# Second to sixth modulation: weighted sums over the row tiles moved from the matmul engine to GpSimd

## The chip, the cores and the metric

The kernel runs on one core of one Trainium2 chip, as one program with one launch. The metric is the device time of that core in microseconds (us). A run's time is a little more than the span of its trace, which goes from the first instruction to the last. The engines are called as the profile calls them: PE is the matmul engine (PEld its weight loads), DVE the vector engine, ACT the scalar engine, POOL is GpSimd, and SP is the engine whose queue issues nearly all transfers.

## The reference

One layer of a diffusion backbone over 512 tokens of width 1024, with a context of 256 tokens. What the change touches is the modulation vector: the conditioning vector `c` goes through silu, is multiplied with a weight matrix of 1024 rows and 6 x 1024 columns, a bias is added, and the 6144 numbers are cut into six vectors of 1024.

```python
def adaln(cond, w_mod, b_mod):
    return jnp.split(jax.nn.silu(cond) @ w_mod + b_mod, 6, axis=-1)
...
sh1, sc1, g1, sh2, sc2, g2 = [m[:, None, :] for m in adaln(c, w_mod[l], b_mod[l])]
csh1, csc1, cg1, csh2, csc2, cg2 = adaln(c_ctx, w_mod[l], b_mod[l])
hx = modulate(rmsnorm(x, norm_attn_g[l]), sh1, sc1)
...                       # latent attention and neighbourhood attention, concatenated, projected: mixed
x = x + g1 * mixed
hx2 = modulate(rmsnorm(x, norm_ffn_g[l]), sh2, sc2)
x = x + g2 * hierarchical_moe(hx2, ...)
```

The first two vectors (shift and scale of the first norm) are needed at once, for the tokens and for the context; the kernel computes them at its start. The other four (g1, sh2, sc2, g2, columns 2048 to 6143) are needed for the tokens alone, and late: g1 when the attention output is projected, sh2 and sc2 before the experts, g2 in the experts. The matrix part for these four is 1024 x 4096 numbers, 16 MB in fp32.

## The kernel before, in words

The stages follow one another: the first modulation, the norms and the input projections (to about 110 us of the trace); neighbourhood attention, with the projections of the next heads mixed in (about 110 to 245 us); latent attention with the output projection (to about 370 us); routing (to about 434 us); sixteen experts; the last sums and the last norm.

The change is in the neighbourhood stage. It is a loop over 32 blocks `b`: four pairs of heads `p`, two heads `u`, four tiles of 128 queries `i`. Each block computes scores (L603, L604, on PE), adds the bias to them and takes the row maximum (L609, L469, on DVE), takes the exponential (L616, on ACT), and one block later turns the probabilities (L625, on PE) and copies them out of PSUM. Between these it pulls pieces of the projections of the next pair (L56 to L58, on PE). In the last eight blocks, and in the turns after them, the pieces are those of the latent attention's values, whose weights `w_ukv`, `w_uq` are loaded there.

In every second block, `mod_rest(n)` does one sixteenth of the rest of the modulation: `n` runs over two halves `r` of 2048 columns and eight tiles `k` of 128 rows. It loads 128 x 2048 weights in two pieces of 512 KB into the `raw` buffers, of which there are three and which all weight loads of this stage share (L179), and issues four matmuls of 512 columns. Their stationary side is `sstat[:, k, :]`, 128 rows by 32 columns with the silu of `c` in column 0 and that of `c_ctx` in column 1; each of the four lands on its own 32 columns of PE's array and its own 32 rows of one PSUM bank. After the eighth tile DVE adds the bias row (L524), and the result goes to `mod_d` in DRAM (L525), from which the later stages read it.

The order of the instructions on each engine is not written out by hand in this stage. A planner takes each engine's instructions in about the order of the code, but lets one go ahead whose inputs it expects to be there earlier; so an engine's queue can differ from the code (SP's does, by far). At run time each queue is in order: an instruction that waits holds everything behind it on its engine.

The buffers of the pool `omp` (two of 128 x 2048 fp32, tags `0` and `1`) hold `qst` and `krs` before this stage. Both are stored to DRAM (L422 `qn_dram`, L410 `kr_dram`), and the buffers are idle then until the latent stage puts `omh` and `oml` in them. `zero` is a tile of zeros that is stored ten times to clear `ya_d` (L774).

Of the kernel before, what the change touches and what calls it, by code (L numbers as in the profile page):

```python
# [37 lines left out]
def hybrid_kernel(tc, nc, x_k, x_q, ctx, cvec, w_mod_a, w_mod_b, b_mod_c, b_mod_r, g_ffn_row,  # L38
# [90 lines left out]
    sm = cst.tile([P, 24], F32, name="sm")  # L129
    eps = cst.tile([P, 1], F32, name="eps")  # L130
    ve.memset(eps, EPS)
    lg = cst.tile([P, 4, 20], F32, name="lg")
    lsh = cst.tile([P, 20], F32, name="lsh")
    idx = cst.tile([P, 2, NE], I32, name="idx")
    wsl = cst.tile([P, NE], F32, name="wsl")
# [41 lines left out]
    def load(src, n=1024):  # L177
        r = raw_tile()
        sy.dma_start(r[:, :n], src)  # L179
        return r  # L180
# [317 lines left out]


    ya_d = tc.dram_tile([T + P, D], F32, name="ya_d")  # L500
    zero = nw.tile([P, 512], F32, name="zero")
    ve.memset(zero, 0.0)


    mod_d = tc.dram_tile([2, 4, 512], F32, name="mod_d")
    modf = mod_d.rearrange("r a b -> r (a b)")
    mod_ps = []

    def mod_rest(n):
        r, k = divmod(n, KT)  # L510
        if k == 0:
            br = nw.tile([P, 512], F32, name="br", tag="br", bufs=1)
            ve.memset(br, 0.0)
            rows = br.rearrange("(a b) n -> a b n", b=32)[:, 0, :]
            sy.dma_start(rows, b_mod_r[r])
            mod_ps[:] = bank(7), br, rows
        ps, br, rows = mod_ps
        ws = [load(w_mod_b[r, k, :, q * 1024:(q + 1) * 1024]) for q in range(2)]
        for g in range(4):
            pe.matmul(ps[g * 32:(g + 1) * 32, :], sstat[:, k, :],  # L520
                      ws[g // 2][:, g % 2 * 512:g % 2 * 512 + 512], start=(k == 0), stop=(k == KT - 1),
                      tile_position=(0, g * 32))
        if k == KT - 1:
            ve.tensor_tensor(br, br, ps, op=OP.add)  # L524
            sy.dma_start(mod_d[r], rows)  # L525

    na_heads, na_w, na_ps = {}, {}, {}

# [149 lines left out]

    blocks = [(p, u, i) for p in range(4) for u in range(2) for i in range(4)]
    na_open(0)  # L680
    for j in range(2):
        for i in range(2):
            na_weights(0, j, i)
# [27 lines left out]
    for b, (p, u, i) in enumerate(blocks):  # L711
        w = b % 8
        if w == 0 and p < 3:
            na_open(p + 1)
        s = na_scores(p, u, i)
        nm = na_max(p, u, i, s)
        if p < 3:
            if w in (3, 5, 7):
                for u_ in range(2):
                    na_part(p + 1, w // 2 - 1, u_, 1)  # L720
            if w == 2:
                na_weights(p + 1, 1, 1)
            if w == 4 and p < 2:
                na_weights(p + 2, 0, 1)
            if w == 6:
                for u_ in range(2):
                    na_bias(p + 1, u_)
        if NS[p][w] > 1:
            pull(1)
        if len(turns) >= (2 if b > 24 else 1):  # L730
            na_turn(*turns.pop(0))
        turns.append((p, u, i))
        na_exp(p, u, i, s, nm)
        if w == 0 and p:
            norm_ = normalise_steps(na_ssum[p - 1], nw, onh[:, p - 1, :], onl[:, p - 1, :])
            next(norm_)
        if i % 2:
            mod_rest(p * 4 + u * 2 + i // 2)
        pull(NS[p][w] - (NS[p][w] > 1))
        if w == 0 and p:  # L740
            norm_.send((na_values(p - 1), bank4(4, 5)))
        if w == 1 and p:
            for _ in norm_:
                pass
        if p < 3:
            if w in (2, 4, 6):
                for u_ in range(2):
                    na_part(p + 1, w // 2 - 1, u_, 0)
            if w == 1:
                na_weights(p + 1, 1, 0)  # L750
            if w == 3 and p < 2:
                na_weights(p + 2, 0, 0)
        if b == 23:
            htp.release()
            ml = pool("ml")
            vv = ml.tile([P, 6, 512], F32, name="vv")
            wkh = ml.tile([P, 2, 512], F32R, name="wkh")
            wkl = ml.tile([P, 2, 512], F32R, name="wkl")
            mp = pool("mp")
            ckq = mp.tile([P, 256], F32, name="ckq")  # L760
            qnl = mp.tile([P, 3, T], F32R, name="qnl")
            qnh = mp.tile([P, 3, T], F32R, name="qnh")
            sy.dma_start(ckq, cpk[:, K_QC:K_R])
            krt = mp.tile([P, T + TC], F32, name="krt")
            sy.dma_start(krt[64:96, :], kr_dram)
            uq = [[mp.tile([P, 768], F32R, name=f"uq{c}{i_}") for i_ in range(2)] for c in range(3)]
            mla_weights(0)
            works = works2
        if b == 24:
            mla_weights(1)  # L770
        if w == 7:
            for n in range(2 * p, min(2 * p + 2, 5)):
                for hf in range(2):
                    sy.dma_start(ya_d[n * P:(n + 1) * P, hf * 512:hf * 512 + 512], zero)  # L774
    for tn in turns:
        pull(1)
        na_turn(*tn)
# [290 lines left out]
    rng3 = pool("rng3", side="right")  # L1068
    add_slots(rng3, M1 - R1 - LD)
    wp = pool("wp", side="right")  # L1070
    gs = wp.tile([P, D], F32, name="gs")
    sh = wp.tile([P, D], F32, name="sh")
    sy.dma_start(gs, modf[1:2, 0:1024].to_broadcast([P, D]))
# [754 lines left out]
def _layout(**n):  # L1828
    n = {k: np.asarray(v) for k, v in n.items()}
    c = np.ascontiguousarray  # L1830
    ck_, qr_ = _tokens()
    x = n["x"][0]
    wm, wi = n["w_mod"][0], n["w_in"][0]
    bm = n["b_mod"][0]
    a = {}
    a["x_k"] = c(x[ck_].reshape(4, P, D))
    a["x_q"] = c(x[qr_].reshape(4, P, D))
    a["ctx"] = c(n["ctx"][0].reshape(2, P, D))
    a["cvec"] = c(np.stack([n["c"][0], n["c_ctx"]], -1).reshape(KT, P, 2).transpose(1, 0, 2))

    wa = wm[:, :2048].reshape(4, 2, P, 2, 4, 256).transpose(4, 0, 2, 1, 3, 5)

    w0 = wm[:, :2048].reshape(2, 4, P, 2, KT, P)[:, :, :, :, 0:2].transpose(4, 0, 2, 1, 3, 5)
    a["w_mod_a"] = np.concatenate([w0.reshape(1, 4, P, 1024), wa.reshape(4, 4, P, 1024)[1:]])
    a["w_mod_b"] = c(wm[:, 2048:].reshape(KT, P, 2, 2048).transpose(2, 0, 1, 3))

    bt = np.repeat(bm[:2048].reshape(2, 4, 2, P).transpose(3, 1, 0, 2).reshape(P, 4, 4), 2, axis=2)
    gt = np.repeat(n["norm_attn_g"][0].reshape(4, 2, P).transpose(2, 0, 1), 2, axis=2)
    a["b_mod_c"] = c(np.concatenate([bt, gt], 2))
    a["b_mod_r"] = c(bm[2048:].reshape(2, 4, 512))  # L1850
    a["g_ffn_row"] = c(n["norm_ffn_g"])
    a["g_fin_row"] = c(n["final_norm_g"][None])
    nk0 = 384 + 512 + 256 + 32
    a["w_v"] = c(wi[:, nk0 + 512:].reshape(4, 2, P, 512).transpose(0, 2, 1, 3).reshape(4, P, 1024))
    a["w_kv"] = c(wi[:, 896:1184].reshape(KT, P, 288).transpose(1, 0, 2).reshape(P, KT * 288))
    a["w_ql"] = c(wi[:, :384].reshape(4, 2, P, 384).transpose(0, 2, 1, 3).reshape(4, P, 768))
    qk = np.stack([wi[:, 384:896].reshape(KT, P, 4, P), wi[:, nk0:nk0 + 512].reshape(KT, P, 4, P)])
    a["w_qk"] = c(qk.transpose(3, 0, 2, 1, 4).reshape(4, 2, P, 1024))
    a["g_q"] = c(n["q_a_norm_g"][0].reshape(3, P).T)
    a["g_kv"] = c(n["kv_a_norm_g"][0].reshape(2, P).T)  # L1860
    a["w_uq"] = c(n["w_uq"][0].reshape(3, P, 768))
    a["w_ukv"] = c(n["w_ukv"][0].reshape(2, P, NH, 2, 64).transpose(0, 1, 3, 2, 4).reshape(2, P, 1024))
    i, qr = np.arange(P)[:, None] // 8, np.arange(P)[:, None] % 8
    j, kr = np.arange(256)[None, :] // 8, np.arange(256)[None, :] % 8
    dc, dr = j - i + 7, kr - qr + 7
    ok = (dc >= 0) & (dc < 31)
    a["rel"] = c(np.where(ok, n["na_rel_bias"][0][:, dr, np.clip(dc, 0, 30)], np.float32(0)))
    wo = n["w_out"][0]
    a["w_out_a"] = c(wo[512:].reshape(2, 2, P, 2, 512).transpose(3, 0, 2, 1, 4).reshape(2, 2, P, 1024))
    a["w_out_b"] = c(wo[:512].reshape(4, P, D))  # L1870
    wr = np.concatenate([n["w_router_group"][0], n["w_router_expert"][0]], 1)
    a["w_r"] = c(wr.reshape(KT, P, 20).transpose(1, 0, 2))
    a["b_r"] = c(np.concatenate([n["b_router_group"], n["b_router_expert"]], 1))
    a["w_gate"] = c(n["w_gate"][0].reshape(NE, 2, 4, P, 512).transpose(0, 1, 3, 2, 4).reshape(NE, 2, P, 2048))
    a["w_up"] = c(n["w_up"][0].reshape(NE, 2, 4, P, 512).transpose(0, 1, 3, 2, 4).reshape(NE, 2, P, 2048))
    a["w_down"] = c(n["w_down"][0].reshape(NE, 2, 2, P, D).transpose(0, 1, 3, 2, 4).reshape(NE, 2, P, 2048))
    a["cpk0"], a["cpk"] = _constants()
    return a
# [23 lines left out]
```

## Time and profile before

| | us |
|---|---|
| median of 3 runs | 741.38 |
| lowest, highest | 739.67, 742.3 |
| the profiled execution | 742.79 |
| its span | 740.6 |
| PE busy | 699.0 (94% of the span) |
| DVE busy | 545.6 (74%) |
| ACT busy | 445.9 (60%) |
| POOL busy | 79.6 (11%) |

A PE that is busy is not a PE at its peak: the ends of matmuls are modelled and overlap. What counts on it is the distance from the start of a group of matmuls to the start of the next. An instruction's idle time is put down to what ended it.

### The profile page before, as it was taken

The page shows a single profiled execution, that of the slowest core. Times are in us where ns is not written, and L with a number is a line of the kernel's source. Part 1 is how long each engine was busy: PE and PEld are TensorE (multiplying, and loading weights), DVE is VectorE, ACT ScalarE, POOL GpSimd, SP SyncE. Part 2 cuts the span into 40 slices and gives each one's busy share as a digit, 9 for nine tenths or more (in the row PEclk, how much of TensorE's full clock was granted, in tenths as well). Part 3 has the DMA queues.
Part 4 walks back from the last instruction along what each step waited for, and adds up shares of the span by engine and source line. Part 5 has one row for each costly group of instructions (what it writes and reads, how often), then busy time and mean ns, then how long its engine had stood idle before and what let it go on. Part 6 is the DMA issues. An engine that isn't in the chain of part 4 may idle for free. (4 is left out here: it accounts for less than half of the span.)

```text
span 740.6 us, 10570 instructions
## 1 busy us (share of the span) xinstructions
PE 699.0 (94%) x3982; PEld 521.0 (70%) x3983; DVE 545.6 (74%) x744; ACT 445.9 (60%) x697; POOL 79.6 (11%) x50
## 2 busy tenths in 40 slices
PE   4999999999989999999999559999999999999995
PEld 3679988777755887867668537777777777777773
DVE  5572466756666695656627758999999999999996
ACT  6452365554545565646644437777777777777773
POOL 1010000000000000000010011222222222221320
PEclk9999999999999999999999759999999999999998
DMA  9931238654556821121179859999999999999672
GB/s 322 408 127 43 86 131 263 220 184 142 169 194 205 284 87 43 63 76 48 58 269 344 325 178 355 387 369 373 360 361 356 379 363 364 364 369 380 261 135 113
DMA packets 39622, 176.95 MB, mean 239 GB/s; under 512 B 5288, under 2 KB 6768, under 8 KB 27280
## 3 DMA queue, kind: packets, MB, share of 16 engines
q1 hardware_dynamic: 35168, 164.24, 60.3%
q0 software_dynamic: 4112, 11.92, 7.5%
q8 instruction: 32, 0.52, 0.3%
q14 instruction: 22, 0.18, 0.1%
q10 hardware_dynamic: 288, 0.08, 0.0%
HBM read 163.00 MB, written 15.32 MB: 241 GB/s over the span
## 5 line engine op out<-in xcount | busy, mean ns | idle before, releaser
L1360 DVE TENSOR_TENSOR el<-ew,eh 128x2048 fp32r<-128x2048 f32 (+1 forms) x106 | 220.5, 2086 | 22.0 <-ACT eh L1357 13.2
L1357 ACT CAST eh<-ew 128x1024 fp32r<-128x1024 f32 x190 | 189.7, 1048 | 43.7 <-PE s L58 29.1
L56 PE MATMUL s<-eh,xh 128*96 128x512 f32 x260 | 104.6, 402 | 0.9 <-ACT xh L61 0.9
L58 PE MATMUL s<-eh,xl 128*96 128x512 f32 x260 | 103.1, 396 | 0.0
L57 PE MATMUL s<-el,xh 128*96 128x512 f32 x260 | 102.5, 394 | 0.0
L1571 POOL DMA_INDIRECT ya_d<-yo,idx x14 | 45.5, 3254 | 140.6 <-DVE yo L1575 140.6
L58 PEld LDWEIGHTS s<-eh,xl 128*96 128x96 f32 x260 | 42.2, 162 | 19.2 <-DVE xl L62 0.6
L56 PEld LDWEIGHTS s<-eh,xh 128*96 128x96 f32 x260 | 42.3, 163 | 18.0 <-ACT xh L61 1.2
L57 PEld LDWEIGHTS s<-el,xh 128*96 128x96 f32 x260 | 42.5, 163 | 17.4 <-DVE el L1360 0.2
L56 PE MATMUL y<-eh,ghh 128*96 128x512 f32 x120 | 48.2, 401 | 0.0
L58 PE MATMUL y<-eh,ghl 128*96 128x512 f32 x120 | 47.3, 394 | 0.0
L57 PE MATMUL y<-el,ghh 128*96 128x512 f32 x120 | 47.2, 393 | 0.0
L469 DVE TENSOR_REDUCE nm<-s 128x1 f32<-128x768 f32 x32 | 30.5, 954 | 19.4 <-PE s L58 19.2
L56 PE MATMUL ps<-wh,hh 128*128 128x512 f32 (+2 forms) x128 | 43.8, 345 | 0.4 <-ACT hh L274 0.3
L58 PE MATMUL ps<-wh,hl 128*128 128x512 f32 (+2 forms) x128 | 43.5, 345 | 0.3 <-DVE hl L276 0.3
L57 PE MATMUL ps<-wl,hh 128*128 128x512 f32 (+2 forms) x128 | 43.3, 341 | 0.0
L1288 POOL MEMSET xg<- 128x1024 f32 x2 | 1.9, 960 | 327.4 <-DMA g<-mod_d 327.4
L56 PE MATMUL ps<-hh,wh 128*128 128x512 f32 (+1 forms) x96 | 36.4, 380 | 0.0
L1246 POOL DMA_INDIRECT xg<-hx_d,idx x16 | 23.3, 1457 | 120.2 <-DVE va L1169 52.2
L937 ACT ACTIVATE pr<-s,nm 128x768 f32<-128x768 f32 x32 | 29.1, 908 | 9.9 <-DVE nm L469 9.4
L58 PE MATMUL ps<-hh,wl 128*128 128x512 f32 (+1 forms) x96 | 34.4, 358 | 0.0
L57 PE MATMUL ps<-hl,wh 128*128 128x512 f32 (+1 forms) x96 | 34.2, 356 | 0.0
(358 smaller groups left out, 1471.8 us busy)
## 6 DMA issues: line engine op xcount, KB each, us to landing
ew<-w_gate SPq DMA_DIRECT2D x32, 1024.0 KB, 8.2
ew<-w_up SPq DMA_DIRECT2D x32, 1024.0 KB, 8.9
ew<-w_down SPq DMA_DIRECT2D x32, 1024.0 KB, 8.8
raw<-w_mod_b SPq DMA_DIRECT2D x32, 512.0 KB, 4.1
wm<-w_mod_a SPq DMA_DIRECT2D x16, 512.0 KB, 10.2
raw<-w_qk SPq DMA_DIRECT2D x8, 512.0 KB
ya_d<-zero SPq DMA_DIRECT2D x10, 256.0 KB, 6.8
raw<-w_v SPq DMA_DIRECT2D x4, 512.0 KB
```

Source lines behind the costliest of these rows:

```text
L56: pe.matmul(ps, lh, rh, start=start, stop=False)
L57: pe.matmul(ps, lh, rl, start=False, stop=False)
L58: pe.matmul(ps, ll, rh, start=False, stop=stop)
L469: ve.tensor_reduce(out=nm, in_=s, axis=AX.X, op=OP.max, negate=True)
L937: ac.activation(pr, s, AF.Exp, bias=nm, accum_out=mla_ssum[h // 2][:, t, h % 2:h % 2 + 1])
L1246: ins = gp.indirect_dma_start(out=xg[e % NX][slice(0, CAP), :], out_offset=None, in_=hx_d, in_offset=bass.IndirectOffsetOnAxis(ap=idx[slic ...
L1288: gp.memset(x_, 0.0)
L1357: ac.copy(wh[:, cs], r[:, cs])
L1360: ve.tensor_tensor(wl[:, cs], r[:, cs], f(wh[:, cs]), op=OP.subtract)
L1571: gp.indirect_dma_start(out=ya_d, out_offset=bass.IndirectOffsetOnAxis(ap=idx[rows, 1, e:e + 1], axis=0), in_=yo[rows, :], in_offset=None, ...
```

## The change

The rest of the modulation is cut otherwise: eight pieces `r` of 512 columns, each in two halves `h` of four row tiles. `mod_rest(n)` now loads one half, 128 x 4 x 512 weights, 1 MB in one transfer, into one of the two `omp` buffers. GpSimd multiplies each of the four tiles of 512 columns with its column of `sstat` (the silu of `c` for those 128 rows, one number per partition), adds the first two tiles to the last two (128 x 1024), and adds what is left to 128 x 512. The first half's sum is the accumulator `macc`; the second half's is added to it. `mod_sum(r)` then has the matmul engine add the 128 rows: a column of ones, taken 32 times, against 4 x 128 columns of the accumulator. DVE adds the bias, and the row goes to `mod_d`, which keeps its flat layout.

The first two halves are asked for ahead of the loop, the other fourteen in every second block up to block 27, the sums in blocks 4, 8, ... 28, and the last sum in block 31. To make room, the tile `lg` moves to a later pool, and `zero` is half as wide and read twice for a store. The weights lie in DRAM in the new order (`w_mod_b`, `b_mod_r`).

```diff
-    lg = cst.tile([P, 4, 20], F32, name="lg")
...
-    zero = nw.tile([P, 512], F32, name="zero")
+    zero = nw.tile([P, 256], F32, name="zero")
...
-    mod_d = tc.dram_tile([2, 4, 512], F32, name="mod_d")
-    modf = mod_d.rearrange("r a b -> r (a b)")
-    mod_ps = []
+    mod_d = tc.dram_tile([8, 4, P], F32, name="mod_d")
+    modf = mod_d.rearrange("(h r) a b -> h (r a b)", h=2)
+    mod_acc = {}
+    one = cst.tile([P, 1], F32, name="one")
+    ve.memset(one, 1.0)
+    ones = one.to_broadcast([P, 32])
 
     def mod_rest(n):
-        r, k = divmod(n, KT)
-        if k == 0:
-            br = nw.tile([P, 512], F32, name="br", tag="br", bufs=1)
-            ve.memset(br, 0.0)
-            rows = br.rearrange("(a b) n -> a b n", b=32)[:, 0, :]
-            sy.dma_start(rows, b_mod_r[r])
-            mod_ps[:] = bank(7), br, rows
-        ps, br, rows = mod_ps
-        ws = [load(w_mod_b[r, k, :, q * 1024:(q + 1) * 1024]) for q in range(2)]
+        r, h = divmod(n, 2)
+        w = omp.tile([P, 4, T], F32, name=f"wb{h}", tag=f"{h}", bufs=1)
+        sy.dma_start(w, w_mod_b[r, h])
+        for k in range(4):
+            gp.tensor_scalar(w[:, k, :], w[:, k, :], sstat[:, 4 * h + k, 0:1], None, op0=OP.mult)
+        gp.tensor_tensor(w[:, 0:2, :], w[:, 0:2, :], w[:, 2:4, :], op=OP.add)
+        if h == 0:
+            acc = mod_acc[r] = nw.tile([P, 512], F32, name="macc", tag="macc", bufs=2)
+            gp.tensor_tensor(acc, w[:, 0, :], w[:, 1, :], op=OP.add)
+        else:
+            gp.tensor_tensor(w[:, 0, :], w[:, 0, :], w[:, 1, :], op=OP.add)
+            gp.tensor_tensor(mod_acc[r], mod_acc[r], w[:, 0, :], op=OP.add)
+
+    def mod_sum(r):
+        acc = mod_acc.pop(r)
+        br = nw.tile([P, P], F32, name="br", tag="br", bufs=1)
+        ve.memset(br, 0.0)
+        rows_ = br.rearrange("(a b) n -> a b n", b=32)[:, 0, :]
+        sy.dma_start(rows_, b_mod_r[r])
+        ps = bank(7)
         for g in range(4):
-            pe.matmul(ps[g * 32:(g + 1) * 32, :], sstat[:, k, :],
-                      ws[g // 2][:, g % 2 * 512:g % 2 * 512 + 512], start=(k == 0), stop=(k == KT - 1),
+            pe.matmul(ps[g * 32:(g + 1) * 32, 0:P], ones, acc[:, g * P:(g + 1) * P], start=True, stop=True,
                       tile_position=(0, g * 32))
-        if k == KT - 1:
-            ve.tensor_tensor(br, br, ps, op=OP.add)
-            sy.dma_start(mod_d[r], rows)
+        ve.tensor_tensor(br, br, ps[:, 0:P], op=OP.add)
+        sy.dma_start(mod_d[r], rows_)
...
     na_open(0)
+    mod_rest(0)
+    mod_rest(1)
...
-        if i % 2:
-            mod_rest(p * 4 + u * 2 + i // 2)
+        if b % 2 and b < 28:
+            mod_rest(2 + b // 2)
+        if b % 4 == 0 and b:
+            mod_sum(b // 4 - 1)
+        if b == 31:
+            mod_sum(7)
...
-                    sy.dma_start(ya_d[n * P:(n + 1) * P, hf * 512:hf * 512 + 512], zero)
+                    sy.dma_start(ya_d[n * P:(n + 1) * P, hf * 512:hf * 512 + 512].rearrange("p (a b) -> p a b", a=2),
+                                 zero[:, None, :].to_broadcast([P, 2, 256]))
...
+    lg = wp.tile([P, 4, 20], F32, name="lg")
```

## Rows read from the trace of the kernel before

**Rows 1.** The page: busy time, share of the span and instructions of each engine.

```profile
PE 699.0 (94%) x3982; PEld 521.0 (70%) x3983; DVE 545.6 (74%) x744; ACT 445.9 (60%) x697; POOL 79.6 (11%) x50
```

**Rows 2.** Busy time by stretch; then granted clock, DMA share, GB/s.

```profile
core 0: us, PE busy (x) PEld busy (x) DVE busy (x) ACT busy (x) POOL busy (x), PEclk, DMA share, GB/s
110.00:122.00 12.00, 12.00 (x67) 10.24 (x67) 8.61 (x16) 6.39 (x12) 0.00 (x0) 1.00 0.78 270
...
122.00:240.00 118.00, 115.29 (x749) 81.00 (x748) 75.60 (x135) 61.39 (x129) 0.00 (x0) 0.99 0.59 192
```

**Rows 3.** Timeline of PE: start, duration, line, shape, idle before it.

```profile
204.72 1.07 PE L520 MATMUL ps<-raw,sstat 128*32 128x512 f32 x8
205.72 0.39 PE L603 MATMUL ps<-kk,qh 128*128 128x256 f32 x1
...
208.17 0.50 PE L56 MATMUL ps<-wh,kvh 128*128 128x512 f32 x1 [1.72 <-ACT wh L61]
...
238.61 1.05 PE L520 MATMUL ps<-raw,sstat 128*32 128x512 f32 x4 [0.61 <-DMA raw<-w_mod_b]
239.60 0.55 PE L625 MATMUL ps<-c,pr 128*128 128x128 f32 x3
...
245.14 0.47 PE L56 MATMUL o<-kvh,wkh 128*128 128x512 f32 x1
```

**Rows 4.** Groups of PE by form, 118 to 242 us.

```profile
L520 PE MATMUL ps<-raw,sstat 128*32 128x512 f32 x128 | 20.2, 605 | 1.0 <-DMA raw<-w_mod_b 0.9
```

**Rows 5.** Timeline of PE in the first modulation.

```profile
25.45 0.65 PE L245 MATMUL ps<-wm,sstat 128*32 128x128 f32 x16
```

**Rows 6.** Busy time by stretch, around 208 us.

```profile
210.00:212.00 2.00, 2.00 (x9) 1.82 (x8) 0.51 (x1) 0.83 (x2) 0.00 (x0) 0.50 0.75 266
212.00:214.00 2.00, 2.00 (x15) 1.33 (x16) 1.51 (x3) 2.00 (x6) 0.00 (x0) 0.71 0.01 2
```

**Rows 7.** Groups of POOL by form: busy us, mean ns, idle before.

```profile
L531 POOL MEMSET ql<- 64x512 f32 x4 | 2.1, 568 | 38.7 <-PE ps L245 38.7
L1288 POOL MEMSET xg<- 128x1024 f32 x2 | 1.9, 960 | 327.4 <-DMA g<-mod_d 327.4
```

**Rows 8.** Timeline of SP's queue.

```profile
105.51 0.34 SPq L410 DMA_DIRECT2D kr_dram<-krs x1
...
111.22 0.33 SPq L422 DMA_DIRECT2D qn_dram<-qst x1
...
200.52 0.38 SPq L179 DMA_DIRECT2D raw<-w_ukv  x1
```

**Rows 9.** Transfers: KB of each, us to landing.

```profile
ew<-w_gate SPq DMA_DIRECT2D x32, 1024.0 KB, 8.2
...
raw<-w_mod_b SPq DMA_DIRECT2D x32, 512.0 KB, 4.1
```

**Rows 10.** Groups of DVE by form, 118 to 242 us.

```profile
L561 DVE TENSOR_TENSOR wl<-raw,wh 128x1024 fp32r<-128x1024 f32 x5 | 6.1, 1221 | 7.2 <-ACT wh L558 7.2
...
L62 DVE TENSOR_TENSOR uq<-raw,uq 128x768 fp32r<-128x768 f32 x3 | 2.9, 952 | 0.0
...
L490 DVE TENSOR_TENSOR onl<-rsb,onh 128x512 fp32r<-128x512 f32 x3 | 2.0, 681 | 0.0
L550 DVE TENSOR_TENSOR bb<-rb,cka 128x256 f32<-128x256 f32 x5 | 2.0, 407 | 0.0
L551 DVE TENSOR_TENSOR bb<-rb,cka 128x256 f32<-128x256 f32 x5 | 2.0, 406 | 0.0
L62 DVE TENSOR_TENSOR wl<-raw,wh 128x512 fp32r<-128x512 f32 x2 | 1.4, 688 | 0.9 <-ACT wh L61 0.9
L62 DVE TENSOR_TENSOR wkl<-raw,wkh 128x512 fp32r<-128x512 f32 x2 | 1.4, 684 | 0.0
...
L62 DVE TENSOR_TENSOR qnl<-raw,qnh 128x512 fp32r<-128x512 f32 x2 | 1.4, 680 | 0.0
```

**Rows 11.** Waits of SP's queue: us in total, times, longest.

```profile
SPq L179 <- PE ps L520: 53.1, 18, 6.7
```

More of the change, by code (lines that the diff above doesn't have):

```diff
@@ L1844, in _layout @@
     a["w_mod_a"] = np.concatenate([w0.reshape(1, 4, P, 1024), wa.reshape(4, 4, P, 1024)[1:]])
-    a["w_mod_b"] = c(wm[:, 2048:].reshape(KT, P, 2, 2048).transpose(2, 0, 1, 3))
+    a["w_mod_b"] = c(wm[:, 2048:].reshape(2, 4, P, 8, 512).transpose(3, 0, 2, 1, 4).reshape(8, 2, P, 4, 512))
     bt = np.repeat(bm[:2048].reshape(2, 4, 2, P).transpose(3, 1, 0, 2).reshape(P, 4, 4), 2, axis=2)
@@ L1849, in _layout @@
     a["b_mod_c"] = c(np.concatenate([bt, gt], 2))
-    a["b_mod_r"] = c(bm[2048:].reshape(2, 4, 512))
+    a["b_mod_r"] = c(bm[2048:].reshape(8, 4, P))
     a["g_ffn_row"] = c(n["norm_ffn_g"])
```

## The prediction

> **What bounds the kernel now.** I read the page first, for the shares: PE is busy nearly throughout and POOL hardly at all [rows 1]. That is an average over stages, so I went to the stretch of the change by windows: from 122 to 240 us PE is busy 115.3 of 118 us, DVE 75.6, ACT 61.4, POOL 0.0 [rows 2]. So in this stage PE sets the end, and what is taken off PE shortens it until another engine, or a wait, comes up. POOL is free for the whole stage, and the transfers take 0.59 of their time.
>
> Then the timeline of PE, for what one step of `mod_rest` costs there. The eight matmul records of a step (each matmul has two) start at 204.72 and the next work starts at 205.72: 1.00 us a step [rows 3]. A step whose two loads come apart is cut in two groups of four, and each of these takes as long: 238.61 to 239.60 [rows 3]. Thirteen steps stand whole in the timeline and three are cut, so 13 + 6 = 19 groups of 1.0 us. The group view agrees: 20.2 us with the modelled tail of about 0.06 us on each group, and 1.0 us of idle time before them, mostly for their weights [rows 4].
>
> The third view is SP's waits: 53.1 us in which a load into a `raw` buffer waited for the matmuls of `mod_rest` to let go of one [rows 11]. Most of it costs nothing, but one place does: the load of `w_ukv` goes out at 200.52 [rows 8], and PE then stands idle for 1.72 us until 208.17 [rows 3]. After that the granted clock is 0.50 from 210 to 212 and 0.71 from 212 to 214 [rows 6], which is the lower of its two levels (1.2 GHz) for some of the time and 2.4 GHz for the rest; at these shares 2 x 0.50 + 2 x 0.29 = 1.6 us are lost.
>
> **What comes off PE.** 19.0 us of groups, 1.0 us of waits before them, and, if `w_ukv` comes earlier, 1.7 + 1.6 us. What is added is eight sums, each of eight records of 128 columns. The first modulation has sixteen such records in 0.65 us with a tail of 0.27 us [rows 5], so a sum is about 0.25 us, and eight are 2.0 us. If nothing else comes up, the stage's end (the first matmul of the latent stage, 245.14 [rows 3]) moves to 245.1 - 19.0 - 1.0 - 3.3 + 2.0 = 223.8, 21.3 us earlier. That is the most that the change can bring.
>
> **What comes onto GpSimd.** For each of the eight pieces: eight multiplications of 512 columns, two additions of 1024, three of 512, thirteen instructions. No row has such an instruction on POOL. The nearest are two fills, 512 columns in 0.568 us and 1024 in 0.960 [rows 7]: 0.766 ns a column and 0.176 us besides. The lower bound takes each instruction as a fill: 11 x 0.568 + 2 x 0.960 = 8.2 us a piece. The upper bound takes each column read or written as a pass by itself, two passes for a multiplication and three for an addition: 0.96, 1.35 and 2.53 us, 8 x 0.96 + 3 x 1.35 + 2 x 2.53 = 16.8 us. Between them, writes go beside reads and two inputs are read one after the other: 8 x 0.57 + 3 x 0.96 + 2 x 1.74 = 10.9 us. To this I add 0.16 us for each of thirteen hand-overs, since most instructions work on what the one before has just written: 13.0 us a piece, which I take, 104 us for eight.
>
> **When GpSimd can begin.** Its first buffer is free when the store of `qst` has landed, which is issued at 111.22; the second after the store of `krs`, issued at 105.51 [rows 8]. A transfer of 512 KB takes 4.1 us here and one of 1 MB in a dense stream 8.2 [rows 9], and the transfers are busy at this point (0.78 [rows 2]). 2.5 us for the store and 5 us for the first half give 118.5, between 111 (the second buffer is worked on first) and 122. From then on a half takes 6.5 us of GpSimd, and its buffer's next load has the other half's 6.5 us to arrive, so the loads are hidden if 1 MB lands in under 6.5 us.
>
> **What the two engines do to each other.** GpSimd would be at work without a break just where DVE has 27 instructions with two inputs from SBUF, 6.1 + 2.9 + 1.4 + 1.4 + 1.4 + 2.0 + 2.0 + 2.0 = 19.2 us together [rows 10]. No row has both on SBUF at once. Between nothing and all of the 19.2 us added to GpSimd's time, I take 8, under half, because many of them will meet GpSimd at a hand-over or waiting.
>
> **The sum.** GpSimd ends at 118.5 + 104 + 8 = 230.5. PE alone would stand before its last sum at about 223.8 - 5.5 - 0.3 = 218, so it waits for GpSimd, there or in smaller parts at the sums before. After the last sum, 0.3 us, PE has what follows the last group now, from 239.60 to 245.14, 5.5 us [rows 3], and a PE that has waited runs some of that at the lower level, 1.6 us as after 208. The stage ends at 230.5 + 0.3 + 5.5 + 1.6 = 237.9, 7.2 us before 245.1. PE goes at its pace from there to the end, so the gain stays: 742.8 - 7.2 = 735.6 for the profiled execution. The median of the runs is 1.4 us below that execution, so 734.2.
>
> **Edits costed at nothing.** The 16 MB of weights are the same bytes, and the transfers have 0.41 of their time free [rows 2]. DVE's bias additions are 128 columns instead of 512, eight instead of two. The stores of zeros have more and smaller pieces, but nothing in this stage reads `ya_d`. The loads of `mod_rest` now wait on SP for GpSimd, two halves back, and hold what is behind them: the loads of the next heads' weights and bias, and `w_ukv`. At 13 us a piece the fourteenth half may be asked for at 118.5 + 6 x 14 = 202.5, so a `w_ukv` behind it goes out about as late as now, 200.5; that alone would keep the wait before 208.17, but it is the same delay as the one that I have counted, not a second one. `lg` is only moved.
>
> **The rivals.**
>
> GpSimd keeps up. Below 12.4 us a piece, all told, GpSimd ends by 218 and PE waits for nothing: up to 21.3 us faster, about 720 to 722. For it speaks that the middle reading without hand-overs is 10.9; against it that all of the 8 us would then have to go too.
>
> The shared path to SBUF decides (the other side). GpSimd and DVE hold each other up for whole instructions. GpSimd then ends at 118.5 + 104 + 19.2 = 241.7, and the stage at 249.1, 4.0 us late. DVE's 27 instructions wait half of a GpSimd instruction each (104 instructions in 104 us, so half of 1.0), 13 us in all; DVE has 42 us to spare in the stage [rows 2], but it stands in the chain from the scores to the exponential, and I let a quarter reach PE, 3 us. That is 7 us slower, 748. It decides from 14.9 us a piece on, all told: (245.1 - 7.4 - 118.5) / 8. The Trainium skill speaks for it: its page SBUF — State Buffer, section SBUF: two separate sides, says that a DVE instruction with two SBUF inputs and a GpSimd instruction that reads SBUF lock each other out for the whole instruction. No run here shows it yet. The page GPSIMD Engine Reference of the Trainium skill, section Elementwise — side-by-side cycle accounting, calls GpSimd about half as fast as DVE for such sums and gives 4497 ns for an addition of 2048 columns; by that, as an estimate, the five additions (3584 columns) of a piece cost 7.9 us where I have 6.4, and the stage would end up to 12 us later than my sum.
>
> GpSimd at the upper bound. 118.5 + 8 x 16.8 + 8 = 260.9, end at 268.3, 23 us slower, 764. Against it: a fill would have to gain nothing from the overlap of reads and writes.
>
> Nothing moves. PE loses 17 us of work and waits as long for sums: all told 14.6 to 15.2 us a piece.
>
> **How the numbers follow.** A change of 0.3%, 2.2 us, is about what a measurement of this kernel can tell from none. GpSimd sets the end, but earlier than now (12.4 to 14.6 us a piece): 0.37, and this is the forecast, 734, with a range of its own from 725 to 739. GpSimd keeps up: 0.17. Within 0.3%: 0.16. Slower by the shared path: 0.24. Slower at the upper bound: 0.06. So faster 0.54, same 0.16, slower 0.30. The range goes from 720, where GpSimd keeps up, to 750, a little above the shared path's 748; the upper bound is left out.
>
> **What would show it.** Right: POOL busy 80 to 115 us between 115 and 235; groups of 512 columns at 0.6 us for a product and about 1 us for a sum; no L520 groups of 1.0 us on PE, small sums of 0.25 us instead; PE idle before the sums, with POOL named as what ended it, and more so towards the end; the latent stage beginning at about 238. Keeping up would show as PE busy throughout and a start at 224. The shared path would show as DVE's instructions with two SBUF inputs beginning late or taking longer than 1.22 us for 1024 columns, and GpSimd's durations spread widely. The prediction is wrong if a piece costs much less or more than 13 us on GpSimd, if the planner puts the sums far from their places in the code, or if SP's queue, held by a load that waits for GpSimd, starves the projections.

## The result and the profile after

The changed kernel takes 810.2 us, median of four runs (809.1 to 811.3), against 740.5 for the kernel before in the same rounds (739.4 to 742.3): 1.094 times as long, interval 1.092 to 1.096. The forecast was 734.2 in a range of 720 to 750. The profiled execution takes 809.1 us at a span of 807.4.

The page of the kernel after, its shares (those of before are in [rows 1]):

```profile
PE 707.2 (88%) x3918; PEld 534.0 (66%) x3919; DVE 554.1 (69%) x757; ACT 446.6 (55%) x697; POOL 255.3 (32%) x154
```

POOL goes from 80 to 255 us. In a window of the changed kernel (columns as in [rows 2]):

```profile
122.00:240.00 118.00, 73.61 (x428) 55.66 (x427) 48.98 (x85) 34.99 (x72) 112.33 (x68) 0.79 0.40 138
```

PE falls from 115.3 to 73.6 us of the same 118, DVE and ACT fall as well, the transfers from 0.59 to 0.40, and PE's granted clock from 0.99 to 0.79. Only POOL is busy nearly throughout, 112.3 us. PE's timeline dates the end of the stage:

```profile
215.68 1.12 PE L641 MATMUL ps<-c,pr 128*128 128x128 f32 x4 [17.52 <-ACT pr L632]
...
313.90 0.48 PE L56 MATMUL o<-kvh,wkh 128*128 128x512 f32 x1
```

The latent stage begins at 313.9 where it began at 245.1 [rows 3]: 68.8 us late. The span grew by 66.8, so all of the loss arises up to this point, and 2.0 us of it come back later.

Groups of POOL by form, 110 to 310 us (busy us, mean ns | idle before):

```profile
L520 POOL TENSOR_SCALAR wb<-wb,sstat 128x512 f32<-128x512 f32 x64 | 101.6, 1603 | 76.5 <-DMA wb<-w_mod_b 76.5
L521 POOL TENSOR_TENSOR wb<-wb 128x1024 f32<-128x1024 f32 x16 | 39.1, 2443 | 1.3
L524 POOL TENSOR_TENSOR macc<-wb 128x512 f32<-128x512 f32 x8 | 14.0, 1750 | 0.6
L526 POOL TENSOR_TENSOR wb<-wb 128x512 f32<-128x512 f32 x8 | 10.8, 1353 | 0.6
L527 POOL TENSOR_TENSOR macc<-macc,wb 128x512 f32<-128x512 f32 x8 | 10.2, 1272 | 0.6
```

175.7 us in eight pieces, 22.0 us a piece: 12.7 for the eight multiplications, 9.3 for the five additions. The prediction took 13.0 all told and held 16.8 for the most that it could be. POOL's timeline gives the undisturbed durations and the ends (the 69.22 us of idle time lie ahead of the stage):

```profile
114.81 6.21 POOL L520 TENSOR_SCALAR wb<-wb,sstat 128x512 f32<-128x512 f32 x4 [69.22 <-DMA wb<-w_mod_b]
121.11 3.21 POOL L521 TENSOR_TENSOR wb<-wb 128x1024 f32<-128x1024 f32 x1
...
125.66 6.20 POOL L520 TENSOR_SCALAR wb<-wb,sstat 128x512 f32<-128x512 f32 x4
...
134.41 2.12 POOL L524 TENSOR_TENSOR macc<-wb 128x512 f32<-128x512 f32 x1
...
295.25 2.35 POOL L521 TENSOR_TENSOR wb<-wb 128x1024 f32<-128x1024 f32 x1
...
299.35 1.26 POOL L527 TENSOR_TENSOR macc<-macc,wb 128x512 f32<-128x512 f32 x1
```

Four multiplications stand 6.3 us from the next instruction's start (114.81 to 121.11): 1.55 us of work each, and hand-overs of under 0.1 us. POOL works from 114.8 to 300.6. The same addition of 1024 columns takes 2.35 us or 3.21, that of 512 takes 1.26 or 2.12: some are held up.

The chain that ended last, from 110 to 320 us, its shares by line:

```profile
by line: POOL wb L520 48.3%; POOL wb L521 18.7%; DMA wb<-w_mod_b 7.3%; POOL macc L524 6.7%; POOL wb L526 5.2%; POOL macc L527 3.6%; PE ps L650 2.0%; issue 1.8%; PE ps L641 0.8%; PE ps L56 0.8%; ACT kh L68 0.7%; PE ps L58 0.6%; PE ps L57 0.6
```

82.5% of it is POOL. But the waits in the same stretch (us in total, times, longest) don't show PE waiting mostly for POOL:

```profile
ACT pr L632 <- DVE nm L468: 51.5, 15, 17.1
...
PE ps L641 <- ACT pr L632: 36.0, 8, 17.5
...
DVE br L533 <- DMA mod_d<-br: 28.8, 3, 17.7
...
PE ps L538 <- POOL macc L527: 20.1, 3, 11.1
DVE br L540 <- DMA br<-b_mod_r: 18.6, 2, 13.7
```

The sums' wait for the accumulator is 20.1 us. More time passes at the probabilities (L641), which wait for the exponential, which waits for DVE's row maximum, and DVE stands before a `br` whose transfer is late. Why it is late, SP's waits and SP's timeline say:

```profile
SPq L518 <- POOL macc L524: 70.8, 7, 14.6
SPq L518 <- POOL macc L527: 54.3, 7, 10.9
```

```profile
195.81 11.60 SPq L518 DMA_DIRECT2D wb<-w_mod_b  x2
207.47 0.42 SPq L178 DMA_DIRECT2D raw<-w_ukv  x1
...
208.47 0.89 SPq L541 DMA_DIRECT2D mod_d<-br  x1
...
217.89 11.66 SPq L518 DMA_DIRECT2D wb<-w_mod_b  x2
229.64 0.54 SPq L535 DMA_DIRECT2D br<-b_mod_r  x1
```

Two loads into POOL's buffers are issued between 195.8 and 207.4, each when POOL lets go of its buffer. Behind them stands the store of a finished bias row (208.47). DVE can clear the one `br` buffer for the next sum only when that store has landed, and stands idle for 17.7 us before it does; the row maximum stands behind the clearing. DVE's timeline:

```profile
148.68 2.52 DVE L577 TENSOR_TENSOR wl<-raw,wh 128x1024 fp32r<-128x1024 f32 x1 [0.71 <-ACT wh L574]
...
179.85 2.89 DVE L489 TENSOR_TENSOR onl<-rsb,onh 128x512 fp32r<-128x512 f32 x1
...
214.04 0.17 DVE L533 MEMSET br<- 128x128 f32 x1 [17.69 <-DMA mod_d<-br]
...
234.19 0.29 DVE L540 TENSOR_TENSOR br<-br,ps 128x128 f32<-128x128 f32 x1 [13.70 <-DMA br<-b_mod_r]
```

PE resumes at 215.68 after 17.5 us (above). The same again 20 us later with the load of a bias row, 229.64 on SP and 234.19 on DVE. The first two rows here show the other effect: 1024 columns in 2.52 us (1.22 in [rows 10]), 512 in 2.89 (0.68), beside POOL's additions.

### The profile page after: what moved, and what is told of

Same layout as the page of the kernel before. It is cut to its first block, busy times and chain, and to the rows that moved or that the text cites. A ratio compares the mean times of both kernels' runs of the same rounds, so it can differ in the third digit from the quotient of the medians.

```text
span 807.4 us, 10559 instructions
## 1 busy us (share of the span) xinstructions
PE 707.2 (88%) x3918; PEld 534.0 (66%) x3919; DVE 554.1 (69%) x757; ACT 446.6 (55%) x697; POOL 255.3 (32%) x154
## 4 chain that ended last, share of the span: by engine, by line
PE 67%; POOL 21%; DMA 4%; DVE 3%; ACT 3%; issue 1%; SPq 0%; DVEq 0%; POOLq 0%; ACTq 0%
POOL wb L520 13%; PE s L56 10%; PE s L58 10%; PE s L57 10%; POOL wb L521 5%; PE y L56 3%; PE y L58 3%; PE y L57 3%; PE ps L58 3%; PE ps L56 3%; PE o L982 3%; PE ps L57 3%; PE tr L973 3%; DMA wb<-w_mod_b 2%; POOL macc L524 2%; POOL wb L526 1%
## 5 line engine op out<-in xcount | busy, mean ns | idle before, releaser
L520 POOL TENSOR_SCALAR wb<-wb,sstat 128x512 f32<-128x512 f32 x64 | 101.6, 1603 | 76.5 <-DMA wb<-w_mod_b 76.5
L641 PE MATMUL ps<-c,pr 128*128 128x128 f32 x128 | 23.2, 311 | 36.0 <-ACT pr L632 36.0
L632 ACT ACTIVATE pr<-ps,nm 128x512 f32<-128x512 f32 x32 | 22.0, 688 | 51.7 <-DVE nm L468 51.5
L641 PEld LDWEIGHTS ps<-c,pr 128*128 128x128 f32 x128 | 17.1, 160 | 44.8 <-ACT pr L632 40.8
```

Of the source, the lines that this page charges most:

```text
L520: gp.tensor_scalar(w[:, k, :], w[:, k, :], sstat[:, 4 * h + k, 0:1], None, op0=OP.mult)
L641: pe.transpose(tr[:, j, :], pr[:, j * P:(j + 1) * P], ident)
```

## The experiments

The theory after the result: the multiplications are mis-sized, POOL sets the end, and the stage follows POOL whatever is waited for. Rivals: the sums' wait makes the loss; SP's held queue makes it by itself; POOL and DVE lock each other out of SBUF. Ratios are against the kernel before in the same rounds.

**The multiplications out.**

```diff
-        for k in range(4):
-            gp.tensor_scalar(w[:, k, :], w[:, k, :], sstat[:, 4 * h + k, 0:1], None, op0=OP.mult)
```

> GpSimd leaves out its 64 multiplications (the weights are added up unweighted) and does the additions alone. In the changed kernel POOL is busy from 114.8 to 300.6 us with 101.6 us of multiplications and 74 us of additions. Theory 1, GpSimd's rate sets the end: 9.3 us a piece, GpSimd is done by about 195, ahead of PE, and the stage ends at PE's pace: 720 to 728 us. Theory 2, the queues: SP's loads wait for GpSimd two halves back and hold DVE's bias row behind them, so a good part of the loss stays: over 760. Theory 3, the shared path to SBUF: the additions are the instructions with two inputs, so most of the holding up stays: 745 to 760.

738.4 us, 0.997 (0.995 to 0.999); the latent stage begins at 242.8. Leaving out 102 us of POOL's work takes away the whole loss of 70, so the multiplications are what the loss hangs on; but the time lies in none of the three ranges. With five additions a piece POOL is done by 221.5, and yet the stage begins only 2.3 us earlier than before the change.

**The sums read zeros.** Nothing on PE waits for POOL.

```diff
-            pe.matmul(ps[g * 32:(g + 1) * 32, 0:P], ones, acc[:, g * P:(g + 1) * P], start=True, stop=True,
+            pe.matmul(ps[g * 32:(g + 1) * 32, 0:P], ones, zero[:, 0:P], start=True, stop=True,
```

> GpSimd does all of its work, but PE adds up a tile of zeros in place of the accumulators, so PE waits for no sum. SP's queue is left as it is: its loads still wait for GpSimd's buffers. Theory 1 in its direct form (PE waits for the accumulators, 41 us in the profile, and everything else follows from that): 720 to 735. Theory 2 (SP's queue, held by those loads, brings weights, bias rows and stores late, at GpSimd's pace): the stage still ends with GpSimd, about 790 to 810.

809.8 us, 1.093 (1.087 to 1.098); the stage begins at 314.8. No gain, as theory 2 had it. (The 41 us of the expectation add 20.1 of PE and 21.0 of its weight loads, which wait side by side: it is one wait of some 20 us.) In this kernel's waits from 110 to 320 us PE's chief one is that for the exponential, and DVE's that for the bias row's store:

```profile
PE ps L641 <- ACT pr L632: 72.1, 7, 22.2
DVE br L533 <- DMA mod_d<-br: 51.9, 5, 17.6
```

**The loads on POOL's own queue.** SP no longer waits for POOL's buffers.

```diff
-        sy.dma_start(w, w_mod_b[r, h])
+        gp.dma_start(w, w_mod_b[r, h])
```

> All as in the changed kernel, but the loads of the halves are issued on GpSimd's own queue, so nothing on SP waits for GpSimd's buffers. Theory 1: PE still waits for the accumulators, GpSimd still takes 22 us a piece: 800 to 815. Theory 2: SP brings weights, bias rows and stores in time, DVE isn't held: 745 to 775.

810.6 us, 1.094 (1.088 to 1.100); 315.5. No gain either, as theory 1 had it: by the waits of this kernel it has gone back to the sums, all eight of them.

```profile
PE ps L538 <- POOL macc L527: 69.0, 8, 12.2
```

**Both.**

> Both of the two before: PE adds up zeros, and the loads of the halves go through GpSimd's own queue. Nothing in the stage waits for GpSimd any more, while GpSimd does all its work. Both theories: PE's pace, 720 to 728, if holding each other up at SBUF costs PE nothing; what lies above 724 or so is the price of the shared path (theory 3), 10 us or more if it matters.

801.7 us, 1.082 (1.076 to 1.088): far from the 720 to 728 expected. PE now begins the latent stage at 239.1, while POOL works until 313.6, and stops there, as its waits show:

```profile
DVE kl L73 <- POOL macc L527: 61.0, 2, 47.7
...
PE o L56 <- DVE kl L73: 47.3, 1, 47.3
```

`kl` reads nothing that POOL writes; it waits for the accumulators' last use, as a tile does that is given their memory. So POOL's end comes to the stage by three ways, and closing two leaves the third. That `kl` lies in the accumulators' memory is read from this wait; a kernel with the two kept apart wasn't run.

**Products alone: the additions out, the multiplications in.**

```diff
-        gp.tensor_tensor(w[:, 0:2, :], w[:, 0:2, :], w[:, 2:4, :], op=OP.add)
-        if h == 0:
+        if h:
...
+        for k in range(4):
+            dst = acc if h and k == 0 else w[:, k, :]
+            gp.tensor_scalar(dst, w[:, k, :], sstat[:, 4 * h + k, 0:1], None, op0=OP.mult)
```

> GpSimd does the 64 multiplications alone and leaves out all additions (PE adds up the rows of the last product of each piece only, so the other row tiles are left out of the sum). GpSimd: about 102 us in all, more than the 74 us of the run without multiplications (738.4 us). Theory 3, additions hold DVE's instructions with two inputs up and multiplications don't: DVE's instructions keep the durations of before (1.22 us for 1024 columns, 0.41 for the bias), PE is waited for less, and the kernel is faster than that run although GpSimd works longer: 722 to 731. If it is not the kind of instruction but GpSimd's time that counts: 738 to 750.

745.7 us, 1.006 (1.003 to 1.008); 250.0. Theory 3's range is missed; the time lies in the other one. The groups of POOL and the first matmul of the latent stage:

```profile
L523 POOL TENSOR_SCALAR wb<-wb,sstat 128x512 f32<-128x512 f32 x56 | 90.3, 1628 | 16.4 <-DMA wb<-w_mod_b 13.8 <-ACT kk L598 2.4 <-POOL wb L523 0.2
L523 POOL TENSOR_SCALAR macc<-wb,sstat 128x512 f32<-128x512 f32 x8 | 12.5, 1562 | 69.1 <-DMA wb<-w_mod_b 69.1
...
250.02 0.48 PE L56 MATMUL o<-kvh,wkh 128*128 128x512 f32 x1
```

POOL's busy time is 102.8 us, 12.9 a piece, almost the 13.0 of the prediction, and POOL ends at 232.3, near the predicted 230.5. No wait of PE for an accumulator shows in its trace. Still the stage begins 12 us later than the predicted 237.9. So the price of a piece is not the only failed step. Three runs below take it up.

**Additions alone, products alone, with nobody waiting**: the two kernels above, each with the loads on POOL's queue and sums of zeros.

> GpSimd does the additions alone (multiplications left out), its loads go through its own queue, and PE adds up zeros: nothing in the stage waits for GpSimd, which is at work for some 80 us. What is left is what its additions do to DVE through SBUF. Theory 3 (a DVE instruction with two inputs and a GpSimd addition hold each other up): DVE's instructions take half as long again or longer, the stage ends at 232 to 238, 728 to 735. If they do nothing to each other: PE's pace, an end at about 224, 720 to 724.

> The same with the multiplications alone (additions left out), one input each, some 102 us of GpSimd. Theory 3: DVE keeps its durations (1.22 us for 1024 columns, 0.41 for the bias), the stage ends at 224 to 229, and the kernel is 5 us or more faster than the run with the additions alone, although GpSimd is at work longer: 720 to 727. If any work of GpSimd slows the stage alike: as slow as the run with the additions or slower, 730 to 738.

Additions alone: 739.4 us, 0.999 (0.996 to 1.002), 242.3. Products alone: 731.2 us, 0.987 (0.984 to 0.990), 234.2. POOL does 77 us of work from 122 to 240 in the first and 110 in the second, and the one with less work costs 8 us more: from 122 to 240 PE is busy 109.0 us at a granted clock of 0.97 in the first, 112.7 at 1.00 in the second. Both are slower than expected (728 to 735 and 720 to 727). Groups of DVE by form, 112 to 245 us, of the additions alone:

```profile
L575 DVE TENSOR_TENSOR wl<-raw,wh 128x1024 fp32r<-128x1024 f32 x6 | 8.3, 1391 | 3.2 <-ACT wh L572 2.3 <-ACT qst L419 0.9
L565 DVE TENSOR_TENSOR bb<-rb,cka 128x256 f32<-128x256 f32 x8 | 6.8, 855 | 0.0
...
L489 DVE TENSOR_TENSOR onl<-rsb,onh 128x512 fp32r<-128x512 f32 x4 | 5.1, 1274 | 1.3 <-ACT onh L488 1.3
```

and of the products alone:

```profile
L573 DVE TENSOR_TENSOR wl<-raw,wh 128x1024 fp32r<-128x1024 f32 x6 | 7.8, 1302 | 3.5 <-ACT wh L570 2.6 <-ACT qst L419 0.9
...
L563 DVE TENSOR_TENSOR bb<-rb,cka 128x256 f32<-128x256 f32 x8 | 4.1, 516 | 0.0
L489 DVE TENSOR_TENSOR onl<-rsb,onh 128x512 fp32r<-128x512 f32 x4 | 3.6, 906 | 3.1 <-ACT onh L488 3.1
```

Against 1221, 407 and 681 ns in [rows 10] the additions lengthen DVE's small sums to about twice, the products by a quarter to a third. So the two engines do hold each other up, in POOL's additions above all. The additions alone with both waits in place began the stage at 242.8 (the run without multiplications), so for them the two waits cost next to nothing; what is left there goes with the work itself.

**Products alone, one wait at a time.** With POOL's own queue but sums that read the accumulator:

> The additions are left out (as in the run of the products alone), the matmul engine's sums read GpSimd's accumulator, and the loads for GpSimd's buffers go through GpSimd's own queue. A piece costs GpSimd 12.9 us here, as the prediction took, and the products alone with all waits in place began the latent stage at 250.0, with nobody waiting at 234.2. If SP's queue held by those loads makes the difference: the stage begins at 234 to 238, 731 to 735 us. If it is the sums' wait for the accumulator: at 248 to 251 again, 744 to 747 us. If each takes half: about 242, 738 us.

749.3 us, 1.012 (1.007 to 1.016); 254.7. With SP's queue but sums of zeros:

> The additions are left out and the matmul engine's sums read zeros instead of GpSimd's accumulator, but the loads stay on SP's queue. The counterpart of the run before. If SP's queue makes the difference: the latent stage begins at 248 to 251, 744 to 747 us. If the sums' wait does: at 234 to 238, 731 to 735 us.

750.9 us, 1.015 (1.011 to 1.019); 253.6. Neither wait's removal helps alone: each run comes out somewhat above the range for the case that the other wait counts, and both are 3.6 to 4.7 us later than with the two waits. The second is the clean one: beside the products alone with nobody waiting its edit differs only in the queue of the loads (the planner orders the queues anew), and the stage begins 19.4 us later, although PE waits for no accumulator and POOL is done at 226. The starts of the latent stage, nobody waiting and then this kernel:

```profile
234.19 0.47 PE L56 MATMUL o<-kvh,wkh 128*128 128x512 f32 x1
...
253.60 0.48 PE L56 MATMUL o<-kvh,wkh 128*128 128x512 f32 x1
```

From the waits of this kernel, SP's last:

```profile
DVE br L529 <- DMA mod_d<-br: 24.5, 3, 9.7
PE ps L637 <- ACT pr L628: 20.5, 6, 8.8
...
ACT wh L570 <- DMA raw<-w_qk: 9.8, 2, 8.8
...
SPq L518 <- POOL wb L523: 61.0, 12, 6.9
```

So loads that are held on SP's queue are enough for the loss. How much of it comes by the bias rows and how much by the late `w_qk` is read from these waits alone: a kernel with only the bias rows on another queue wasn't run. Nor is it settled why this stage begins 3.6 us later than the one whose sums read the accumulator. The first of the two isn't as clean: with its own queue POOL ends later, at 245.4, since it begins at 119.7 instead of 113.4 and issues its sixteen loads itself, 0.56 us each. From there the stage takes the 9.3 us that a wait for POOL's end gives (7.4 in the prediction's sum).

**Half of the pieces back on PE.** Pieces 0 to 3 are done by PE through `raw`, pieces 4 to 7 by POOL, their halves spread over the stage.

```diff
+        if b in GH:
+            mod_rest(10 + GH.index(b))
+        if b % 2:
+            mod_pe(b // 2)
+        if b in GS:
+            mod_sum(4 + GS.index(b))
```

> Pieces 0 to 3 on PE as half the loads through the shared buffers, pieces 4 to 7 on GpSimd, which has 88 us of work then and is done by about 205, ahead of its sums (blocks 8, 16, 24 and 31). Theory 1 (GpSimd's rate, 22 us a piece, decides): half of the work fits, and the kernel is faster than before: about 9 us of PE and 4 us of waits less, some of it given back to DVE's hold-ups: 728 to 737. If a GpSimd at work slows the stage whatever its rate: 742 or more.

761.4 us, 1.028 (1.021 to 1.034); 261.1. Theory 1 misses: POOL is done at 208, but SP's timeline shows the same hold:

```profile
152.30 11.96 SPq L518 DMA_DIRECT2D wb<-w_mod_b  x2
164.35 0.53 SPq L562 DMA_DIRECT2D mod_d<-br  x1
```

The same with the loads on POOL's queue:

> The half-and-half kernel (761.4 us, its GpSimd done by 208 us of the trace) with GpSimd's four pieces loaded through its own queue. Theory 2 for that kernel (SP stood 12 us at a load that waited for GpSimd's buffer, and w_qk and the halves for PE came late behind it): the loss goes, 728 to 740. If the loss came from the shared path or from GpSimd's rate: 755 to 765.

741.6 us, 1.000 (0.998 to 1.002); 246.4, just above the range of theory 2. The hold on SP cost some 20 us here; what half of the pieces takes off PE is just eaten up by the rest.

**The product in the additions' form**: one instruction with two inputs, the factor repeated along the columns.

```diff
-        for k in range(4):
-            gp.tensor_scalar(w[:, k, :], w[:, k, :], sstat[:, 4 * h + k, 0:1], None, op0=OP.mult)
+        gp.tensor_tensor(w, w, sstat[:, 4 * h:4 * h + 4, 0:1].to_broadcast([P, 4, T]), op=OP.mult)
```

> The four multiplications of a half become one instruction with two inputs over 2048 columns, the second of them the column repeated 512 times. At the rate of the additions (2.39 us for 1024 columns) it takes 4.8 us where the four take 6.2: 11 us less in eight pieces would be 2.8 us each, 22 us in all. Theory 1: the time falls by as much, to 785 to 792. If the queues or the shared path set it: 800 to 812, the shared path even slower.

Its products in the groups of POOL:

```profile
L519 POOL TENSOR_TENSOR wb<-wb,sstat 128x2048 f32<-128x2048 f32 x16 | 59.2, 3700 | 77.6 <-DMA wb<-w_mod_b 76.3 <-issue 1.3
```

773.3 us, 1.043 (1.035 to 1.051); 278.8. Faster than expected, since the product takes 3.7 us and not 4.8. The same products in 59.2 us instead of 101.6, and the time falls by 37 us: most of the 42 us that POOL saves, the stage saves.

**A constant factor** (1.5 instead of the column of `sstat`), one run:

> The changed kernel with a constant factor in place of the column of the silu (so the sums are weighted with a constant). If it is the factor read from SBUF that makes a multiplication of 512 columns take 1.55 us on GpSimd: about 0.6 to 0.9 us, GpSimd's work falls by 40 to 60 us and the kernel to 745 to 770. If a multiplication costs that whatever its factor: 1.55 us and about 810.

Its multiplications in the groups of POOL:

```profile
L520 POOL TENSOR_SCALAR wb<-wb 128x512 f32<-128x512 f32 x64 | 95.7, 1520 | 75.9 <-DMA wb<-w_mod_b 75.9
```

801.7 us, 8.5 less than the changed kernel, 5.9 of them in the multiplications. 1.52 us instead of 1.60 on average: reading the factor isn't what makes the multiplication long.

**The idle buffers, but with PE's matmuls.** The loads go to the two `omp` buffers as in the change; PE does all of the sums, 16 matmuls of 128 columns (32 records) for half a piece, and POOL nothing.

```diff
+        for k in range(4):
+            for g in range(4):
+                pe.matmul(ps[g * 32:(g + 1) * 32, 0:P], sstat[:, 4 * h + k, :], w[:, k, g * P:(g + 1) * P],
+                          start=(h + k == 0), stop=(h == 1 and k == 3), tile_position=(0, g * 32))
```

> All sums back on PE, eight row tiles of four times 128 columns to a piece, but the loads go to the two idle buffers, 1 MB each, and no longer through the three shared ones. It does the moving of buffers alone. If the wait for w_ukv (1.7 us of idle PE and 1.6 us of lower clock) and the waits for the halves (1.0 us) go away, and 8 records of 128 columns cost 0.22 where 8 of 512 cost 1.0: 733 to 738. If the shared buffers cost nothing: 740 to 743.

737.7 us, 0.995 (0.992 to 0.998); 243.2. This is the fastest kernel here that leaves nothing out, and faster than both: loads in buffers of their own, with the smaller matmuls and the loads' other places in the loop, are worth some 0.5%; the move to POOL is what costs.

## Why the prediction was wrong

**The step that failed: "What comes onto GpSimd".** The prediction's own terms, beside what was measured, for the stage's end (237.9 predicted, 313.9 measured, 76.0 late):

| term | predicted | measured |
|---|---|---|
| POOL begins | 118.5 | 114.8 |
| eight pieces with hand-overs | 104 | 169.8 |
| held up by DVE | 8 | 8.7 |
| POOL waits for its loads | 0 | 7.3 |
| from POOL's end to the latent stage | 7.4 | 13.3 |

The pieces: 16 x (6.20 + 2.35) + 24 x 1.26 = 167.0 us at undisturbed durations, and 2.8 of hand-overs. The hold-up is what the groups take above that, 175.7 - 167.0. The loads are 76.5 us of waiting less the 69.2 ahead of the stage, and the hand-overs what is left of 300.6 - 114.8. The pieces make 65.8 of the 76.0 us. Within a piece: multiplications 12.4 against 4.6, additions 8.5 against 6.4, hand-overs 0.35 against 2.1.

The price of a column was taken from fills [rows 7], and the "upper bound" was no bound: it let each column that is read or written take as long as a fill's. Additions respect it (1.26 us for 1.35; 2.35 for 2.53); a multiplication takes 1.55 us where it allowed 0.96. Nothing in the trace of before had POOL compute, so the honest upper end was open, and the rival at 764, with a chance of 0.06, was the nearest to what came. The removal of the multiplications and the cheaper product show that this price is the main cause.

**The second failed step: "it is the same delay as the one that I have counted, not a second one"**, said of loads that wait for POOL on SP's queue. With the price of a piece near the predicted one (products alone, 12.9) the stage still began at 250.0, with no wait for an accumulator in its trace, and at 253.6 with sums of zeros. From POOL's end to the latent stage the first of these takes 17.7 us (232.3 to 250.0), where the prediction's sum has 7.4. The prediction names the next heads' weights and bias behind those loads, but works out `w_ukv` alone. It did not follow the two small transfers that the change itself puts behind those loads eight times, the bias row's load and its store, to the single `br` buffer, to DVE's row maximum and so to ACT and PE. So with a price near the predicted one the forecast of a gain fails as well: 745.7, slower by 0.6%, though inside the range. It was named as a way to be wrong ("if SP's queue ... starves the projections") and given no price.

**The ceiling of 21.3 us was too high.** With nobody waiting and only the products on POOL, PE still begins the latent stage at 234.2, not at 223.8. In that kernel PE's largest idle time, in its groups from 122 to 234 us, and one of the sums, cut in two groups, in its timeline:

```profile
L615 PE MATMUL ps<-kk,qh 128*128 128x256 f32 x40 | 12.1, 316 | 2.8 <-ACT pr L628 2.8
...
223.35 0.41 PE L534 MATMUL ps<-zero,one 128*32 128x128 f32 x2
...
225.00 0.42 PE L534 MATMUL ps<-zero,one 128*32 128x128 f32 x6
225.35 0.50 PE L56 MATMUL ps<-wh,kvh 128*128 128x512 f32 x1
```

A group takes 0.35 us to the next start (225.00 to 225.35), and so does a whole sum, where the prediction took 0.25. Two of the eight sums are cut in two, so there are ten groups: about 3.5 us, not 2.0. PE is idle 4.4 us of the 112, nearly all of it behind ACT's exponential. And PE is 1.9 us later before any of this (its first matmuls of 256 columns come at 117.15, and at 115.29 before the change). Some 2.6 us of the difference of 10.4 are not told apart.

**The rival of the shared path** had its mechanism right and was too small to decide. The additions alone cost 8 us more than the products alone with less work on POOL, beside the 70 us of the loss. The Trainium skill, SBUF — State Buffer, section SBUF: two separate sides, states the lock between a DVE instruction with two SBUF inputs and a POOL instruction that reads SBUF. The 2.89 us for 0.68 beside an addition agree with it, the 1.30 for 1.22 beside the products hardly.

**What held.** PE's groups of 1.0 us are gone. POOL's beginning, the size of the hold-up (8 was a choice between nothing and 19.2, so that it came at 8.7 is in part luck), the sign of every wait that was listed as a sign of trouble (PE idle with POOL as its releaser, late DVE instructions) came as described; the rest of the kernel kept its length within 2 us.

## What to carry to other kernels

An engine that has no such work in the trace has no price in it either: fills on the same engine came near for its additions here and far off for its multiplications, so a bound made from them is none; measure one instruction first, or leave the range open on that side. When a transfer is made to wait for a slow engine, list everything behind it on its queue, the small bias rows and stores above all, and follow each to the single buffer and the in-order engine that it stops. And a late engine can reach the critical one by several ways, data, queue and reused memory: that taking one wait away changes nothing doesn't mean that it costs nothing.

## What the runs showed of the hardware

- On POOL a multiplication of 128 x 512 fp32 by one number per partition takes 1.55 us undisturbed, longer than an addition of two such tiles (1.26); on average it takes 1.60, and 1.52 with a constant. No other width was run, so how much of this an instruction costs whatever its width is not known. As a product of two inputs with a repeated factor, 2048 columns take 3.7 us on average: 0.92 us for 512.
- The additions came out near what the page GPSIMD Engine Reference of the Trainium skill, section Elementwise — side-by-side cycle accounting, gives: 4497 ns there for 2048 columns, 2.35 us here for 1024.
- The granted clock of PE was 0.79 from 122 to 240 us after the change, so PE stood at the lower of its two levels (1.2 GHz, not 2.4) for part of that time, where it was 0.99 before [rows 2]; PE had been idle for 44 of these 118 us. Behind the wait of 17.5 us that ended at 215.68, matmuls of 512 columns take 0.63 us, and 0.40 later on.
